# Layer 0 front: rotated q stored once and doubled by its load, keys of both heads in one transpose, v split two blocks at a time, retention scores on 128 rows

## The chip, the cores and the metric

The kernel runs on one core of a Trainium2 chip. The metric is the device time of one execution in microseconds (us). The engines are TensorE (PE; its weight loads are PEld), VectorE (DVE), ScalarE (ACT), GpSimd (POOL) and SyncE (SP, which here only issues DMAs). Work of one engine runs in the order of its queue; engines wait for one another through semaphores.

## The reference

A two-layer encoder on two sequences, 1024 and 512 tokens of 1024 features, all float32: twelve blocks of 128 tokens in all. Layer 0 has two branches from one projection, layer 1 has windowed attention. Only layer 0 is touched here:

```python
z = rmsnorm(x, g) @ w_in
qa, ka, va, ga, qb, kb, vb, gb = split(z)          # 512,128,128,512 | 256,256,512,512 columns
# mixer A: 8 query heads, 2 key/value heads, dim 64, dense attention
qa = rotate_pairs(rmsnorm(qa per head, gain0), ang) * 64**-0.5
ka = rotate_pairs(rmsnorm(ka per head, gain1), ang)
oa = softmax(qa @ ka.T) @ va                       # per head
# mixer B: retention, 4 heads, key dim 64, value dim 128, chunks of 128 tokens
s  = (qb @ kb.T) * decay                           # inside a chunk
ob = rmsnorm(s @ vb + (qb * q_decay) @ state)      # forward and backward scans summed
x  = x + concat(silu(ga) * oa, silu(gb) * ob) @ w_out
```

## The kernel before, in words

Tokens are taken in blocks of 128, four blocks make a group (three groups), two blocks a pair (six pairs). Products that need float32 accuracy are made from a high and a low part (`split`, L109 to L118: ACT writes the high part, DVE the rest).

**Order.** The program first loads x and projects keys and values of mixer A for all twelve blocks (`kv_raw`, tiles `zkv` of tag E). Then for each pair it runs eight pieces of the q projection of head group 0 (`q_pieces_a`), `kv_pair` for the rotary embedding of the keys, and after every second pair `kv_group`. Mixer B (`retention`, `retain`) follows, four heads by two sequences, twelve parts of four blocks. Attention of mixer A (`pipeline`, `prep_a`, `front_a`) comes last, with the q projection of head group 1, the bias table and the gates as filler (`fill_a`). In the filler the q tiles `zq` are taken from the gate weights' ring (`stage`, tag `wg`, four buffers); in the front they come from tag E. The program is laid out by a planner that simulates the engines (`schedule_with_timeline_sim=True`) and so chooses the order of each engine's queue; DMAs named here go through SP's queue but for the loads of split keys and values, which POOL issues.

**Rotary step.** `rope_norm` squares a pair on ACT, sums it on DVE (L389), makes 1/rms on POOL (L103), scales on DVE (L391), multiplies by the swapped sine on POOL (L394, two instructions), by the cosine on DVE (L397), and adds the two on DVE (L400). For q the caller hands in the outputs: for each of the two blocks, `qd` tiles of tag Q in which each head's 64 columns stand twice, so a pair has four adds of 128x256, and each block is stored as 512 columns (L448). For keys there are two adds of 128x128.

**Attention's q.** `prep_a` loads one block of 512 columns (L725), transposes four 128x128 squares, so that rows 0 to 63 and 64 to 127 hold the same query, and splits them into `qh` and `ql`. The key tile holds the high part on one half of its rows and the low part on the other, so that one product sums over both. There are 24 units, the loads in order of the units.

**Keys and values.** `kv_group` does each key/value head by itself: four transposes of a 128x64 slice into a PSUM tile, ACT and DVE make the high and low keys, and for each block one ACT copy and one DVE subtraction of 128x64 split v. Results go to DRAM (L470).

**Retention scores.** For each part `qk` (q beside k) is transposed by four transposes; ACT copies rows 0 to 63 to `qT` and rows 64 to 127 to `kT` (L555, L556), both tiles of 64 rows, and the score product `pss` runs with 64 rows of the array; `kv` and `po` products use 128.

Of the kernel before, what the change touches and what calls it, by code (L numbers as in the profile page):

```python
# [8 lines left out]
F32 = mybir.dt.float32  # L9
# [27 lines left out]
def trunk_kernel(ctx, tc, x, xT, wab, woab, wc, woc, gT, qkg, ret, sink, relb, fng,  # L37
# [15 lines left out]
    def buf(tag, name, n=None, dt=F32):  # L53
        t = wk.tile([P, SIZE[tag]], dt, tag=tag, name=name, bufs=BUFS[tag])
        return t if n is None else t[:, :n]
# [4 lines left out]
    def ps_t(name):  # L60
        return pp.tile([P, 512], F32, tag="s", name=name, bufs=5)
# [107 lines left out]
    def transpose(o, i):  # L169
        return nc.tensor.transpose(o, i, ident)  # L170
# [163 lines left out]
    x1T_d, x2T_d = scratch("x1T"), scratch("x2T")  # L334
    q_d = [[dr.tile([P, 512], F32, name=f"qd{g}_{b}")[:] for b in range(NB)] for g in range(2)]
    brow_d = dr.tile([16, 512], F32, name="browd")[:]
# [3 lines left out]

# [1 line left out]
    ident = const.tile([P, P], F32, name="ident")  # L342
# [20 lines left out]

# [1 line left out]
    dma(out=g_sb, in_=gT)  # L365
# [18 lines left out]

    def rope_norm(z, tb, nh, pos, tab, outs):
        tb = tb.rearrange("p (b h d) -> p b h d", b=2, h=nh)
        nc.scalar.activation(tb, z, AF.Square)
        ss = small("ssa", 8)[:, :2 * nh]
        nc.vector.tensor_reduce(ss.rearrange("p (b h) -> p b h", b=2), tb, AX.X, ALU.add)  # L389
        r = rstd_of(ss, 64, 2 * nh).rearrange("p (b h) -> p b h", b=2)  # L390
        nc.vector.tensor_tensor(z, z, r.unsqueeze(3).to_broadcast([P, 2, nh, 64]), ALU.mult)  # L391
        cosb, sinb = tab[:, 0, pos:pos + 2, :], tab[:, 1, pos:pos + 2, :]
        for f in range(2):
            nc.gpsimd.tensor_tensor(  # L394
                tb[:, :, :, f * 32:f * 32 + 32], z[:, :, :, (1 - f) * 32:(2 - f) * 32],
                sinb[:, :, f * 32:f * 32 + 32].unsqueeze(2).to_broadcast([P, 2, nh, 32]), ALU.mult)
        nc.vector.tensor_tensor(z, z, cosb.unsqueeze(2).to_broadcast([P, 2, nh, 64]), ALU.mult)  # L397
        for j in range(2):
            for o in outs(j):
                nc.vector.tensor_tensor(o, z[:, j], tb[:, j], ALU.add)  # L400

# [29 lines left out]
    def q_pieces_a(g, w, tab, filler):  # L431
        for p in PAIRS if filler else range(NB // 2):
            b = 2 * p
            ps = (ps_p if filler else ps_any)("psq")
            for j in range(2):
                for k in range(KT):
                    proj_tm_k(ps[:, j * CW:(j + 1) * CW], w, b + j, k)
                    if k % 2 and (j, k) != (1, KT - 1):
                        yield
            z, tb = stage("zq") if filler else (buf("E", "zq"), buf("H", "tbq"))  # L440
            for j in range(2):
                nc.scalar.activation(z[:, j * CW:(j + 1) * CW], ps[:, j * CW:(j + 1) * CW], AF.Copy,
                                     scale=rs[:, b + j:b + j + 1])
            qd = [buf("Q", "qdw").rearrange("p (h c d) -> p h c d", h=4, c=2) for _ in range(2)]
            rope_norm(z.rearrange("p (b h d) -> p b h d", b=2, h=4), tb, 4, b % 8, tab,
                      lambda j: [qd[j][:, :, c, :] for c in range(2)])
            for j in range(2):
                dma(out=q_d[g][b + j], in_=qd[j].rearrange("p h c d -> p (h c d)"))  # L448
            yield

    def kv_pair(p):
        z = kv_raw[p]
        for j in range(2):
            nc.scalar.activation(z[:, j], z[:, j], AF.Copy, scale=rs[:, 2 * p + j:2 * p + j + 1])
        k = z[:, :, 0]
        rope_norm(k, buf("H", "tbk", 256), 2, (2 * p) % 8, rk, lambda j: [k[:, j]])

    def kv_group(t):
        for i in range(2):
            kk, vv = (buf("Q", n, None, F32R) for n in ("ks", "vs"))  # L460
            pt = ps_t("ptk")
            for j in range(GB):
                z = kv_raw[(t * GB + j) // 2][:, j % 2]
                transpose(pt[0:64, j * P:(j + 1) * P], z[:, 0, i, :])
                vb = vv[:, j * P:(j + 1) * P]
                nc.scalar.activation(vb[:, 0:64], z[:, 1, i, :], AF.Copy)
                nc.vector.tensor_tensor(vb[:, 64:128], z[:, 1, i, :], vb[:, 0:64].bitcast(F32), ALU.subtract)
            split(kk[0:64], kk[64:128], pt[0:64], None)
            for n, v in (("ak", kk), ("av", vv)):
                dma(out=group((sp_d[n, i, 0], sp_d[n, i, 1]), t), in_=v.bitcast(F32))  # L470
# [26 lines left out]

# [1 line left out]
    ropeb = buf("S4", "ropeb").rearrange("p (f b d) -> p f b d", f=2, b=8)  # L499
# [22 lines left out]
    def retention(h, w, b0, b1):  # L522
# [7 lines left out]
        for i0 in parts:  # L530
# [21 lines left out]
            for j in range(GB):  # L552
                transpose(pt[:, j, :], qk[:, j, :])
            qT, kT = v4(buf("H", "qT"))[:64], v4(buf("H", "kT"))[:64]
            nc.scalar.activation(qT, pt[0:64], AF.Copy)  # L555
            nc.scalar.activation(kT, pt[64:128], AF.Copy)  # L556
            qfb = v4(buf("Q", "qfb"))
            for i in range(2):
                nc.vector.tensor_tensor(qfb[64 * i:64 * i + 64], qT,
                                        qdec[:64, h, i, :].unsqueeze(1).to_broadcast([64, GB, P]), ALU.mult)  # L560
# [59 lines left out]

# [1 line left out]
    class Back:  # L622
# [50 lines left out]
    def pipeline(units, prep, front, cap, frees, rate, fill, hook, before=None):  # L673
        """Software pipeline: the scores of later units run beside the products of this one, as far as
        the buffers of the exponentials (cap of them) reach."""
        n = len(units)
# [45 lines left out]
    def prep_a(u):  # L722
        g, b = u
        qd = buf("Q", "qd")
        dma(out=qd, in_=q_d[g][b])  # L725
        pt = ps_t("ptq")
        for h in range(4):
            transpose(pt[:, h * P:(h + 1) * P], qd[:, h * P:(h + 1) * P])
        qh, ql = buf("Q", "qh", None, F32R), buf("Q", "ql", None, F32R)
        split(qh, ql, pt, None)  # L730
        return qh, ql
# [70 lines left out]

# [1 line left out]
    def fin_fm(t, k, y, rb):  # L804
# [47 lines left out]

# [1 line left out]
    wkv = load_w(wc, 0, "w")  # L854
# [38 lines left out]

# [1 line left out]
    k_c, v_c = {0: (KH, KL)}, {0: (V,)}  # L895
# [108 lines left out]

# [1 line left out]
    def fin_out(t, k, y, rb):  # L1006
# [128 lines left out]
```

## Time and the profile before

| what | value |
| --- | --- |
| median of three timed runs | 1546.78 us (1539.06 to 1547.49) |
| profiled execution: span from its first to its last instruction | 1541.9 us |
| PE busy | 1467.9 us (95%) |
| DVE busy | 1061.1 us (69%) |
| ACT busy | 714.0 us (46%) |
| POOL busy | 804.7 us (52%) |
| mean granted TensorE clock | 0.985 |

A timed run holds the span and what lies around it; the profiled execution's own time stands beside the timed runs only through its span, which is 4.9 us under their median. Busy shares are averages over stages with different limits, and matmuls are pipelined, so a busy PE need not be one at its peak. The granted clock is a share of 2.4 GHz: 0.5 is the lower level of 1.2 GHz.

### The profile page before, as it was taken

The numbers are of one execution on the slowest core, as the hardware profiler recorded it, in microseconds if no ns is written. First come the engines' busy times: TensorE is split into PE (matmuls) and PEld (weight loads), VectorE is DVE, ScalarE is ACT, GpSimd is POOL, SyncE is SP. The second block draws the span as 40 slices with busy tenths as digits, with TensorE's granted clock in tenths as the row PEclk, the third lists the DMA queues.
The fourth block names the chain that finished last, engine by engine and source line by source line (L and its number), as shares of the span: only waits on it lengthen the run. The fifth ranks groups of instructions, "written<-read, shape, count | busy, mean of one in ns | idle before, by whom it ended". The sixth has DMA issues, their size and how long they took to land.

```text
span 1541.9 us, 26034 instructions
## 1 busy us (share of the span) xinstructions
PE 1467.9 (95%) x8746; PEld 1277.2 (83%) x8746; DVE 1061.1 (69%) x2488; ACT 714.0 (46%) x1768; POOL 804.7 (52%) x1040
## 2 busy tenths in 40 slices
PE   7989999989999999999998999999999999988897
PEld 7988999987888888778777998888888888766677
DVE  6596455578667667877888327677777767898554
ACT  3632222245455555655653235556556556555102
POOL 7783334257456374887896414442522432567433
PEclk9998999999999999999999999999999999999999
DMA  9441011224421132654563422112213211567773
GB/s 334 155 154 52 19 45 49 64 85 140 138 73 59 48 110 73 217 166 130 153 218 115 124 78 78 52 57 56 80 49 93 61 53 52 169 211 235 242 247 123
DMA packets 112662, 179.54 MB, mean 116 GB/s; under 512 B 12880, under 2 KB 34000, under 8 KB 112528
## 3 DMA queue, kind: packets, MB, share of 16 engines
q1 hardware_dynamic: 110512, 172.37, 35.6%
q0 software_dynamic: 2016, 5.51, 1.2%
q8 instruction: 69, 1.13, 0.3%
q14 instruction: 65, 0.53, 0.1%
HBM read 125.63 MB, written 56.39 MB: 118 GB/s over the span
## 4 chain that ended last, share of the span: by engine, by line
PE 65%; DVE 12%; DMA 8%; POOL 5%; issue 4%; ACT 2%; SPq 1%; POOLq 0%; DVEq 0%; ACTq 0%
PE psg L89 16%; PE psq L89 10%; PE psb L89 8%; PE po L89 8%; PE pte L170 6%; PE pso L89 4%; PE sc L89 3%; PE s L89 3%; PE pskv L89 2%; DMA wraw<-in_woc 2%; DVE xl L118 1%; DVE w L137 1%; DVE nm L782 1%; DMA wraw<-in_woab 1%; DVE el L112 1%
## 5 line engine op out<-in xcount | busy, mean ns | idle before, releaser
L89 PE MATMUL psg<-xh,wg 128*128 128x512 f32 x768 | 261.6, 399 | 1.4 <-POOL wg L137 1.2
L112 DVE TENSOR_TENSOR el<-pte,eh 128x512 fp32r<-128x512 f32 x288 | 196.6, 684 | 56.7 <-ACT eh L111 29.6
L107 POOL TENSOR_SCALAR ec<-ec,rl 128x384 f32<-128x384 f32 (+1 forms) x192 | 109.0, 582 | 233.0 <-DVE rl L997 77.1
L111 ACT ACTIVATE eh<-pte 128x512 fp32r<-128x512 f32 x288 | 169.4, 596 | 119.6 <-PE po L89 66.4
L89 PE MATMUL pso<-xh,w 128*128 128x512 f32 x512 | 179.8, 409 | 9.8 <-DVE w L137 4.3
L89 PEld LDWEIGHTS psg<-xh,wg 128*128 128x128 f32 x768 | 143.7, 188 | 29.7 <-POOL wg L137 1.6
L107 POOL TENSOR_SCALAR e<-e,rl 128x512 f32<-128x512 f32 x160 | 114.6, 728 | 81.7 <-DVE rl L793 23.8
L89 PE MATMUL psg<-xl,wg 128*128 128x512 f32 x384 | 151.1, 393 | 0.0
L992 ACT ACTIVATE ec<-ec,nm 128x384 f32<-128x384 f32 (+1 forms) x192 | 109.6, 572 | 85.6 <-DVE nm L990 80.8
L790 ACT ACTIVATE e<-s,nm 128x512 f32<-128x512 f32 x160 | 108.9, 687 | 75.3 <-DVE nm L787 56.1
L136 POOL TENSOR_SCALAR w<-wraw 128x512 fp32r<-128x512 f32 x116 | 78.7, 680 | 117.7 <-DMA wraw<-in_woc 35.2
L782 DVE TENSOR_REDUCE nm<-s 128x1 f32<-128x512 f32 x160 | 107.5, 682 | 34.3 <-PE s L89 34.0
L89 PE MATMUL psq<-xh,w 128*128 128x512 f32 x384 | 130.1, 397 | 0.6 <-DVE oT L655 0.6
L89 PEld LDWEIGHTS pso<-xh,w 128*128 128x128 f32 x512 | 96.1, 191 | 34.7 <-DVE w L137 7.8
L986 DVE CUSTOM_DVE_ANT_0 ec<-sc,bias,sink_s 128x384 f32<-128x384 f32 (+1 forms) x192 | 105.2, 568 | 20.3 <-PE sc L89 17.4
L89 PE MATMUL pso<-xl,w 128*128 128x512 f32 x256 | 102.0, 399 | 3.3 <-DVE xl L118 3.3
L170 PEld LDWEIGHTS pte<-ident,e 128*128 128x128 f32 x640 | 78.4, 142 | 20.5 <-ACT e L790 1.7
L170 PE MATMUL pte<-ident,e 128*128 128x128 f32 x640 | 94.6, 275 | 0.8 <-ACT e L790 0.6
L137 POOL TENSOR_TENSOR w<-wraw,w 128x512 fp32r<-128x512 f32 x68 | 90.5, 1335 | 1.8
L89 PEld LDWEIGHTS psq<-xh,w 128*128 128x128 f32 x384 | 71.8, 188 | 14.4 <-PE po L89 0.9
L89 PEld LDWEIGHTS psg<-xl,wg 128*128 128x128 f32 x384 | 72.3, 188 | 13.2
L89 PE MATMUL pskv<-w,xh 128*128 128x256 f32 x384 | 73.3, 293 | 9.0 <-ACT xh L117 6.7
(225 smaller groups left out, 3981.8 us busy)
## 6 DMA issues: line engine op xcount, KB each, us to landing
wraw<-in_woab SPq DMA_DIRECT2D x48, 256.0 KB, 3.3
wraw<-in_woc SPq DMA_DIRECT2D x48, 256.0 KB, 3.6
wraw<-in_wab SPq DMA_DIRECT2D x44, 256.0 KB, 3.3
wraw<-in_wc SPq DMA_DIRECT2D x36, 256.0 KB, 3.2
xt<-in_xT SPq DMA_DIRECT2D x24, 256.0 KB, 5.3
xb<-in_x SPq DMA_DIRECT2D x24, 256.0 KB, 4.9
qd<-qdw SPq DMA_DIRECT2D x24, 256.0 KB, 2.0
qd<-qd SPq DMA_DIRECT2D x24, 256.0 KB, 3.1
```

The costliest lines, as they stand in the source:

```text
L89: i = nc.tensor.matmul(ps, lhsT=lhsT, rhs=rhs, start=start, stop=stop)
L107: nc.gpsimd.tensor_scalar(o, i, s, 1.0, ALU.mult, ALU.mult)
L111: nc.scalar.activation(hi, src, AF.Copy)
L112: nc.vector.tensor_tensor(lo, src, hi.bitcast(F32), ALU.subtract)
L118: nc.vector.scalar_tensor_tensor(lo, src, scale, hi.bitcast(F32), ALU.mult, ALU.subtract)
L136: nc.gpsimd.tensor_scalar(w[:, 0, :], raw, 1.0, 1.0, ALU.mult, ALU.mult)
L137: (lo or nc.gpsimd).tensor_tensor(w[:, 1, :], raw, w[:, 0, :].bitcast(F32), ALU.subtract)
L170: return nc.tensor.transpose(o, i, ident)
L782: nc.vector.tensor_reduce(nm2[:, c:c + 1] if nh == 2 else nm[:, h:h + 1], s, AX.X, ALU.max, negate=True)
L790: nc.scalar.activation(eh[c], ss[c], AF.Exp, bias=nm[:, h:h + 1], accum_out=l[:, h, c:c + 1])
L986: nc.vector.tensor_tensor_reduce(es[h][:, :nk], s, bias[h][:, bo:bo + nk], 1.0, sink_s[:, 4 * c + h:4 * c + h + 1], ALU.add, ALU.max, mx[: ...
L992: nc.scalar.activation(es[a][:, :nk], es[a][:, :nk], AF.Exp, bias=nm[:, a:a + 1], accum_out=l[:, a:a + 1])
```

## The change

Four edits, all in layer 0. (1) `rope_norm` adds in place, in one instruction for the whole pair. q is stored from its own tile as 256 columns a block, and `prep_a` loads it twice, into the two 64-column halves of each head. (2) `kv_group` transposes the keys of both heads of a block at once and takes one PSUM tile for both. The second head's high part now goes to rows 64 to 127 and its low part to rows 0 to 63. (3) v is split for two blocks by one ACT and one DVE instruction. (4) `qT` and `kT` have 128 rows: `qT` is the whole transposed tile (q above, k below), and the lower half of `kT` is set to zero by POOL, so that the scores are the same.

```diff
-    q_d = [[dr.tile([P, 512], F32, name=f"qd{g}_{b}")[:] for b in range(NB)] for g in range(2)]
+    q_d = [[dr.tile([P, CW], F32, name=f"qd{g}_{b}")[:] for b in range(NB)] for g in range(2)]
...
-    def rope_norm(z, tb, nh, pos, tab, outs):
+    def rope_norm(z, tb, nh, pos, tab):
...
-        for j in range(2):
-            for o in outs(j):
-                nc.vector.tensor_tensor(o, z[:, j], tb[:, j], ALU.add)
+        nc.vector.tensor_tensor(z, z, tb, ALU.add)
...
-            qd = [buf("Q", "qdw").rearrange("p (h c d) -> p h c d", h=4, c=2) for _ in range(2)]
-            rope_norm(z.rearrange("p (b h d) -> p b h d", b=2, h=4), tb, 4, b % 8, tab,
-                      lambda j: [qd[j][:, :, c, :] for c in range(2)])
+            z4 = z.rearrange("p (b h d) -> p b h d", b=2, h=4)
+            rope_norm(z4, tb, 4, b % 8, tab)
             for j in range(2):
-                dma(out=q_d[g][b + j], in_=qd[j].rearrange("p h c d -> p (h c d)"))
+                dma(out=q_d[g][b + j], in_=z[:, j * CW:(j + 1) * CW])
             yield
...
-        rope_norm(k, buf("H", "tbk", 256), 2, (2 * p) % 8, rk, lambda j: [k[:, j]])
+        rope_norm(k, buf("H", "tbk", 256), 2, (2 * p) % 8, rk)
 
     def kv_group(t):
+        ks = [buf("Q", "ks", None, F32R) for _ in range(2)]
+        vs = [buf("Q", "vs", None, F32R) for _ in range(2)]
+        pt = ps_t("ptk")
+        for j in range(GB):
+            z = kv_raw[(t * GB + j) // 2][:, j % 2]
+            transpose(pt[:, j * P:(j + 1) * P], z[:, 0].rearrange("p h d -> p (h d)"))
         for i in range(2):
-            kk, vv = (buf("Q", n, None, F32R) for n in ("ks", "vs"))
-            pt = ps_t("ptk")
-            for j in range(GB):
-                z = kv_raw[(t * GB + j) // 2][:, j % 2]
-                transpose(pt[0:64, j * P:(j + 1) * P], z[:, 0, i, :])
-                vb = vv[:, j * P:(j + 1) * P]
-                nc.scalar.activation(vb[:, 0:64], z[:, 1, i, :], AF.Copy)
-                nc.vector.tensor_tensor(vb[:, 64:128], z[:, 1, i, :], vb[:, 0:64].bitcast(F32), ALU.subtract)
-            split(kk[0:64], kk[64:128], pt[0:64], None)
-            for n, v in (("ak", kk), ("av", vv)):
+            r0, r1 = 64 * i, 64 - 64 * i
+            split(ks[i][r0:r0 + 64], ks[i][r1:r1 + 64], pt[r0:r0 + 64], None)
+            for p in range(2):
+                v = kv_raw[t * 2 + p][:, :, 1, i, :]
+                vb = vs[i][:, p * CW:(p + 1) * CW].rearrange("p (b s d) -> p b s d", b=2, s=2)
+                nc.scalar.activation(vb[:, :, 0], v, AF.Copy)
+                nc.vector.tensor_tensor(vb[:, :, 1], v, vb[:, :, 0].bitcast(F32), ALU.subtract)
+            for n, v in (("ak", ks[i]), ("av", vs[i])):
...
-            qT, kT = v4(buf("H", "qT"))[:64], v4(buf("H", "kT"))[:64]
-            nc.scalar.activation(qT, pt[0:64], AF.Copy)
-            nc.scalar.activation(kT, pt[64:128], AF.Copy)
+            qT, kT = v4(buf("H", "qT")), v4(buf("H", "kT"))
+            nc.gpsimd.memset(kT[64:128], 0.0)
+            nc.scalar.activation(qT, pt, AF.Copy)
+            nc.scalar.activation(kT[0:64], pt[64:128], AF.Copy)
...
         qd = buf("Q", "qd")
-        dma(out=qd, in_=q_d[g][b])
+        q4 = qd.rearrange("p (h c d) -> p h c d", h=4, c=2)
+        for c in range(2):
+            dma(out=q4[:, :, c, :], in_=q_d[g][b].rearrange("p (h d) -> p h d", h=4))
```

## Rows read from the trace of the kernel before

**Rows 1.** The page's busy times, share of the span and instructions by engine.

```profile
PE 1467.9 (95%) x8746; PEld 1277.2 (83%) x8746; DVE 1061.1 (69%) x2488; ACT 714.0 (46%) x1768; POOL 804.7 (52%) x1040
```

**Rows 2.** Windows: length, busy PE, PEld, DVE, ACT, POOL, granted clock, DMA share, GB/s.

```profile
70.00:116.00 46.00, 41.22 (x328) 39.98 (x327) 44.02 (x102) 15.59 (x50) 38.55 (x48) 0.96 0.43 144
116.00:130.00 14.00, 10.57 (x52) 9.68 (x51) 8.66 (x23) 4.41 (x12) 3.48 (x13) 0.65 0.15 57
...
160.00:200.00 40.00, 40.00 (x337) 39.48 (x337) 21.97 (x47) 9.09 (x18) 15.36 (x30) 1.00 0.15 45
...
330.00:340.00 10.00, 9.40 (x55) 8.91 (x55) 8.10 (x13) 2.56 (x6) 6.71 (x6) 0.74 0.36 111
```

**Rows 3.** Waits of PE from 60 to 130 us: total us, times, longest.

```profile
PE ptk L170 <- DVE zkv L400: 4.7, 4, 1.6
PE ptq L170 <- DVE vs L467: 2.2, 1, 2.2
PE kv L89 <- DVE kfb L549: 1.3, 1, 1.3
```

**Rows 4.** Chain that ended last, up to 420 us: start us, us, what.

```profile
70.92 1.43 DVE qdw L400 x4
...
322.06 1.67 DVE qdw L400 x5
...
324.33 1.00 DVE qdw L400 x3
...
359.29 1.76 DVE qdw L400 x4
...
367.88 2.22 DVE qdw L400 x4
```

**Rows 5.** DVE groups by shape, 60 to 125 us: busy us, mean ns, idle before.

```profile
L400 DVE TENSOR_TENSOR qdw<-zq,tbq 128x256 f32<-128x256 f32 x24 | 9.0, 433 | 0.1
L467 DVE TENSOR_TENSOR vs<-zkv,vs 128x64 fp32r<-128x64 f32 x24 | 5.8, 299 | 0.1
L397 DVE TENSOR_TENSOR zq<-zq,tab 128x512 f32<-128x512 f32 x6 | 5.7, 957 | 1.4 <-POOL tbq L394 1.3
...
L400 DVE TENSOR_TENSOR zkv<-zkv,tbk 128x128 f32<-128x128 f32 x12 | 4.2, 392 | 0.0
```

**Rows 6.** The same chain in mixer B, one part.

```profile
148.83 0.89 PE kv L89 x8
...
151.99 1.08 PE pss L89 x8
```

**Rows 7.** Waits of PE from 320 to 800 us, the longest.

```profile
PE pto L170 <- DVE on L591: 5.2, 1, 5.2
```

**Rows 8.** POOL's timeline: a memset of mixer B, a gate weight's split.

```profile
160.82 0.28 POOL L525 MEMSET stt<- 64x128 f32 x1 [0.98 <-PE po L89]
...
370.25 0.62 POOL L136 TENSOR_SCALAR wg<-wraw 128x512 fp32r<-128x512 f32 x1 [0.76 <-POOL e L107]
```

**Rows 9.** DMA: packets, MB, share in 353.5:356.3 and 345.5:347.8; then landing us.

```profile
q1 hardware_dynamic: 288, 0.13, 16.5%
...
q1 hardware_dynamic: 223, 0.42, 49.5%
...
qd<-qdw SPq DMA_DIRECT2D x24, 256.0 KB, 2.0
qd<-qd SPq DMA_DIRECT2D x24, 256.0 KB, 3.1
```

**Rows 10.** Timeline: q loads on SP's queue, their transposes on PE.

```profile
332.78 0.38 SPq L725 DMA_DIRECT2D qd<-qd  x1
338.43 2.56 SPq L725 DMA_DIRECT2D qd<-qd  x2
...
336.21 0.60 PE L170 MATMUL ptq<-ident,qd 128*128 128x128 f32 x4
341.33 0.63 PE L170 MATMUL ptq<-ident,qd 128*128 128x128 f32 x4
```

More of the change, by code (lines that the diff above doesn't have):

```diff
@@ L553, in retention @@
                 transpose(pt[:, j, :], qk[:, j, :])
-            qT, kT = v4(buf("H", "qT"))[:64], v4(buf("H", "kT"))[:64]
-            nc.scalar.activation(qT, pt[0:64], AF.Copy)
-            nc.scalar.activation(kT, pt[64:128], AF.Copy)
+            qT, kT = v4(buf("H", "qT")), v4(buf("H", "kT"))
+            nc.gpsimd.memset(kT[64:128], 0.0)
+            nc.scalar.activation(qT, pt, AF.Copy)
+            nc.scalar.activation(kT[0:64], pt[64:128], AF.Copy)
             qfb = v4(buf("Q", "qfb"))
             for i in range(2):
-                nc.vector.tensor_tensor(qfb[64 * i:64 * i + 64], qT,
+                nc.vector.tensor_tensor(qfb[64 * i:64 * i + 64], qT[:64],
                                         qdec[:64, h, i, :].unsqueeze(1).to_broadcast([64, GB, P]), ALU.mult)
```

## The prediction

> **What bounds the kernel now.** I read the busy times first [rows 1]. PE is busy 95% of the span, so a change can pay in three ways: by taking work off PE, by removing one of its few waits, or by keeping its clock up. Next come the windows [rows 2]. From 160 to 200 us, in retention, PE is busy for all 40.00 us at full clock: there only PE's own work counts. From 70 to 116 us it is different. DVE is busy 44.02 of 46 us and PE 41.22, so DVE sets the pace, and POOL with 38.55 us is not far behind. From 116 to 130 us PE idles and the granted clock is 0.65, that is, much of the stretch ran at 1.2 GHz; what PE did before that fall was to wait. PE's waits from 60 to 130 us sum to 4.7 + 2.2 + 1.3 = 8.2 us, every one for DVE: for the key adds (L400), the v splits (L467) and a product that stands behind them on DVE [rows 3]. The chain that ended last confirms it: it runs through DVE, with one pair's four q adds as a piece of 1.43 us [rows 4]; the front has six pairs. The same q adds of head group 1 are on the chain again between 322 and 370 us, in four pieces that sum to 1.67 + 1.00 + 1.76 + 2.22 = 6.65 us [rows 4]. PE's longest wait after 320 us, 5.2 us, is in that stretch, for a DVE instruction that was queued behind eight of these adds [rows 7], and the clock is 0.74 right after it [rows 2].
>
> **The change part by part.** The sum is made against the profiled execution.
>
> *Adds of q, front.* Four adds cost 1.43 us [rows 4]. One add of 128x512 is not in the trace in this form. Doubling the 128x256 spacing gives 0.72 us; the cosine product of the same shape and engine took 957 ns in the mean, stretched where POOL worked beside it [rows 5]. So a pair saves 0.47 to 0.71 us, six pairs 2.8 to 4.3; I take 3.9, nearer the doubling, because the 128x256 adds (433 ns mean) are hardly stretched. *Key adds:* twelve of 392 ns become six that cost what a 128x256 add costs, 433 ns [rows 5]: 4.7 less 2.6 is 2.1 at most; as such instructions overlap a little I take 1.3, floor 0.4. *v split:* 24 of 299 ns become twelve of 128x128, at 392 ns by the nearest row [rows 5]: 7.2 less 4.7 is 2.5; I take 1.9, floor 1.1. ACT loses twelve copies too, which costs nothing and gains nothing, since it is busy 15.59 of 46 us [rows 2].
>
> DVE loses 7.1 us in the front by this, bounds 4.3 to 8.9. The most that PE can get is its 8.2 us of waits [rows 3]. POOL has 46 - 38.55 = 7.5 us of room [rows 2], and the chain is not on DVE all the time, so I take 6.0 us. The twelve transposes saved shorten PE too, but where it waits that is nothing; if the waits are gone, twelve at 0.11 us (an eighth of the 0.89 us of eight passes, [rows 6]) make 1.3, which I leave to the upper bound. What is late next is POOL's 1/rms and sine products.
>
> *Clock after the front.* From 116 to 130 us, 35% of 14 us is 4.9 us lost to the lower level [rows 2]. If the gaps before it shrink enough, all comes back; if one remains that is long enough, none. I take half, 2.4, with 0 and 4.9 as ends.
>
> *Scores on 128 rows.* A part's eight `pss` passes take 1.08 us of the chain, eight `kv` passes of the same size on 128 rows 0.89 [rows 6]. I price the new form like `kv`: 0.19 for each of twelve parts is 2.3 us, and as PE is full there [rows 2] it comes through. Floor 0, if the spacing comes from something else than the rows; upper bound 3.4, with some 0.1 us at the entry of each. The ACT copy of 128 rows instead of 64 has the same 512 columns: nothing. The memset: POOL's nearest is 64x128 in 0.28 us [rows 8]; four times the columns make at most 1.1 us, and POOL is busy 15.36 of 40 us there [rows 2], so nothing while its queue has that room. Behind it in POOL's queue stand the sine products of the next part; without the cover it would cost up to 12 x 1.1 = 13 us, which needs PE to wait for each part, and PE waits for none there.
>
> *q adds of group 1.* Of the 6.65 us on the chain [rows 4], four pairs at 0.72 to 0.96 remain: 2.8 to 3.8 us gained, 3.3 taken. The other two pairs are off the chain: nothing. On the other side, `z` is now the source of the store. Its buffer in the gate weights' ring is free not after the add but when the store has landed, 2.0 us later [rows 9]. The last gate weight's split starts at 370.25, right after the last add ends at 370.10 [rows 4, 8]. With a shorter add ending near 368.7 and 2.0 us of store, and 0.1 for the issue, it starts at 370.8: 0.6 us lost, 2.0 at worst.
>
> *The loads.* The stores halve, off the path. A load becomes two DMAs of 512 pieces of 256 bytes. From the windows [rows 9], a 512-byte packet took 16.5% of 16 engines for 2.8 us over 288 packets, 26 ns, and a 2 KB packet 49.5% of 16 for 2.3 us over 223, 82 ns. Two DMAs make 66 packets an engine, semaphore writes included (16 of the packets of each DMA): 1.7 us at 26 ns against 9 x 82 = 0.7 now. The second issue adds 0.4 us [rows 10]. So landing is 1.4 us later; ends 0.8 (17 ns, on the line through both rows) and 5.1 (82 ns). I take 26 ns, the nearest row. Two loads are tight: issued at 332.78 and 338.43, transposed at 336.21 and 341.33 [rows 10], 3.4 and 2.9 us; one before them has about as much, the later ones more. As the second of these two landed within 2.9 us, say 2.5, the new one needs 3.9: PE would wait about 0.5 and 1.0, the earlier one 0.2. I take 1.0 us lost; the planner can move the rest behind filler.
>
> A rule speaks against this edit. The Trainium skill, page DMA: Bandwidth & Descriptors, section Specifications, puts the least transfer for full rate at 512 bytes; below it the DMA engine reads, modifies and writes. No row here has packets of 256 bytes of data, so no run shows it yet; by the rule the sum is that of the second rival below, by the row the one that follows.
>
> The sum: 6.0 + 2.4 + 2.3 + 3.3 - 0.6 - 1.0 = 12.4 us. 1541.9 - 12.4 = 1529.5 us of span; the span lies 4.9 us under the median of the runs shown, and with it the time is 1534 us.
>
> **The rivals.** 0.5% of 1546.78 is 7.7 us, which is about what a measurement of this kernel can tell from no change; so faster means under 1539.0, slower over 1554.5.
>
> *DVE is relieved and POOL or the latency of the chain holds the pace.* For it: POOL's room of 7.5 us is little more than what DVE gives up, and a pair's rotary step goes to and fro between both. Against: PE waits for DVE alone. Then the front gains about 2, the clock nothing, the rest 4.0: 6 us, 1541.
>
> *Small pieces cost twice.* If a 256-byte piece takes 52 ns, twice the nearest row, an engine needs 3.4 us, and landing is 3.1 us later, 5.6 after the issue. The three tight loads then make PE wait 1.9 + 2.2 + 2.7 = 6.8 us instead of the 1.0: 12.4 - 5.8 = 6.6, 1540 us. For it: the shape. Against: the engines are idle around those loads. It is the case that the rule of the Trainium skill, page DMA: Bandwidth & Descriptors, section Specifications, would make.
>
> *Slower: the planner's new order.* The change moves every instruction from 70 us on, and the planner lays all queues anew. What a bad order costs is seen at 325 us: one instruction of DVE behind eight adds, 5.2 us of PE [rows 7] and 2.6 us of clock after it (26% of 10 us, [rows 2]), 7.8 in all. One more such stall in attention leaves 4.6 of the gain, two end 3 us slower than before; from three on it is over the bound: 12.4 - 23.4, 1558 us. For it: the sum is only 0.8% of a run whose order is chosen by a simulation. Against: after 375 us PE's waits are few and short, filler stands ready, and the shorter adds remove what made the one stall.
>
> *More than the sum.* All 8.2 us of PE's waits, 4.9 of clock, 3.4 of scores, and most of the stall at 325 us: some 21 us, 1526.
>
> **How the numbers follow.** Forecast 0.52, with its own range 1527 to 1540; POOL or latency holds 0.20; small pieces cost twice 0.08; the planner's stalls 0.13 (0.10 of them beyond the bound, the rest within it); more than the sum 0.07. Faster: 0.48 of the forecast, 0.07, and 0.05 of the two rivals around 1540, 0.60. Slower: 0.10, and 0.03 for stalls on top of the POOL case, 0.13. Same: the other 0.27. The range is 1523 to 1550: it holds the forecast, both rivals near 1540, more than the sum, and one or two stalls.
>
> **What would show it.** In the profile after: one L400 add a pair of 0.7 to 0.95 us, six fewer key adds; PE waits from 60 to 130 us down from 8.2 to about 2 and the first `pss` some 6 us earlier or more; the clock from there on at 1.00, or still near 0.65 over some 14 us; `pss` pieces at 0.89 instead of 1.08; the first attention units 3 us earlier again relative to retention's end; q loads landing in about 4 us, and no PE wait on `ptq` over 1 us. Wrong it would be if POOL is busy without gaps from 70 to 110 us, if PE waits for the q loads, or if new waits of PE by the 5 us appear after 320 us.

## The result, and the profile after

The changed kernel takes 1532.28 us (median of five, 1528.44 to 1537.83) against 1543.35 us for the kernel before, timed beside it (five, 1539.06 to 1547.49): a ratio of 0.9929, 95% interval 0.9902 to 0.9955, some 11 us or 0.7% faster. Timed again with other versions it took 1534.73 us, ratio 0.9938 (0.9926 to 0.9951). The profiled execution took 1532.67 us with a span of 1530.9, so 1.8 us lie around the span; the span fell by 11.0.

First the page's busy times of the changed kernel, the counterpart of [rows 1].

```profile
PE 1457.4 (95%) x8734; PEld 1271.2 (83%) x8734; DVE 1045.1 (68%) x2434; ACT 714.1 (47%) x1756; POOL 809.5 (53%) x1052
```

PE has twelve passes less, DVE 54 instructions and 16 us, POOL the twelve memsets. The windows (length, busy PE, PEld, DVE, ACT, POOL, granted clock, DMA share, GB/s) answer to [rows 2]:

```profile
70.00:116.00 46.00, 41.60 (x343) 40.79 (x341) 39.50 (x71) 15.50 (x41) 43.99 (x55) 1.00 0.31 104
116.00:130.00 14.00, 11.19 (x94) 10.75 (x93) 12.06 (x30) 6.28 (x15) 3.29 (x11) 1.00 0.21 77
```

The two fullest engines of the front have changed places: DVE fell from 44.02 to 39.50 us of 46, POOL rose from 38.55 to 43.99. From 116 to 130 us the granted clock is 1.00 where it was 0.65. In the kernel before, PE was at the lower level of 1.2 GHz for the first 7 us of retention, after a stretch in which it was busy for 3.47 of 6.90 us, as its own windows show:

```profile
116.00:122.90 6.90, 3.47 (x20) 2.81 (x18) 4.50 (x11) 4.41 (x12) 2.18 (x9) 0.80 0.31 115
122.90:130.00 7.10, 7.10 (x33) 6.87 (x33) 4.16 (x12) 0.00 (x0) 1.30 (x5) 0.50 0.00 0
```

PE's waits from 60 to 130 us (us in total, times, longest), the counterpart of [rows 3]:

```profile
PE ptk L170 <- DVE zkv L398: 4.4, 4, 1.8
PE ptq L170 <- DVE qk L547: 1.7, 1, 1.7
PE kv L89 <- DVE kfb L550: 1.1, 1, 1.1
```

They sum to 7.2 us and not to the 2 that I expected; before they were 8.2. The chain that ended last shows what it runs over (start, us, what):

```profile
86.08 0.87 DVE zq L398
...
91.23 1.37 POOL tbk L394 x2
92.60 3.17 POOL wg L137 x2
95.78 1.86 POOL rstd L103
...
104.14 0.69 DVE zq L398
...
108.68 0.83 DVE zkv L398
```

A pair's q add is one piece of 0.69 to 0.87 us where four took 1.43 [rows 4]. But the chain now runs over POOL: sine products, the split of a retention weight that stands between them (L137, 3.17 us) and 1/rms. Summed over its pieces, POOL carries 12.85 us of the chain from 72.5 to 109.5; in the kernel before it was 4.96 us from 72.5 to 111. The DVE groups of 60 to 125 us (busy us, mean ns, idle before) answer to [rows 5]:

```profile
L397 DVE TENSOR_TENSOR zkv<-zkv,tab 128x256 f32<-128x256 f32 x6 | 5.3, 885 | 0.4 <-POOL tbk L394 0.4
...
L469 DVE TENSOR_TENSOR vs<-zkv,vs 128x128 fp32r<-128x128 f32 x12 | 4.6, 417 | 0.2
L398 DVE TENSOR_TENSOR zq<-zq,tbq 128x512 f32<-128x512 f32 x6 | 4.6, 764 | 0.1
...
L398 DVE TENSOR_TENSOR zkv<-zkv,tbk 128x256 f32<-128x256 f32 x6 | 3.3, 555 | 0.1
```

The q adds fell from 9.0 to 4.6 us, the v splits from 5.8 to 4.6, the key adds from 4.2 to 3.3: 6.5 us less, against the 7.1 of the prediction. At the same time the key's cosine product (L397), which the change doesn't touch, went from 474 to 885 ns in the mean; q's product on the same line went the other way, from 957 to 772 ns, and q's scaling (L391) from 943 to 777. What that depends on is taken up in the last section. In retention the same chain shows one part:

```profile
142.59 0.89 PE kv L89 x8
...
145.75 0.89 PE pss L89 x8
146.64 5.27 PE psb L89 x44
```

The piece of the scores takes 0.89 us, as `kv` does (before 1.08, [rows 6]). The 44 passes behind them take 5.27; in the kernel before the same piece, `psb` x44 at 153.07, took 5.47. How these two prices come about is shown with e3 and e4. POOL's timeline has the new memset, 0.52 us, between two sine products:

```profile
110.14 0.52 POOL L556 MEMSET kT<- 64x512 f32 x1
```

PE's waits from 304 to 739 us, attention, of which [rows 7] gave the longest:

```profile
PE pto L170 <- DVE on L593: 4.0, 1, 4.0
...
PE ptq L170 <- DMA qd<-qd: 1.3, 1, 1.3
PE s L89 <- DVE el L112: 1.1, 2, 0.9
PE po L89 <- DVE oT L657: 0.7, 1, 0.7
```

The stall of 5.2 us is one of 4.0. The other three are not among the waits of the kernel before in that stage. In turn one of its waits behind the adds, of 1.5 us, is gone:

```profile
PE po L89 <- DVE el L112: 1.5, 1, 1.5
```

The loads of q answer to [rows 9, 10]: a window of 325 to 327 us that holds small packets alone (989 packets, 0.25 MB), then the median times to landing (KB each, us), then SP's issues (ns least/median/most):

```profile
q1 hardware_dynamic: 989, 0.25, 54.1%
```

```profile
qd<-qd SPq DMA_DIRECT2D x48, 128.0 KB, 3.1
...
qd<-zq SPq DMA_DIRECT2D x24, 128.0 KB, 1.8
```

```profile
L729 SPq DMA_DIRECT2D qd<-qd x48: 523/617/5236, 281.7 to 717.2; - x48
```

54.1% of 16 engines for 2 us over 989 packets is 17.5 ns for one of 256 bytes, near the lower end (17 ns) that I had put down. A load lands in 3.1 us as before; its issue takes SP 0.62 us, twice a block, instead of 0.38 once.

### The profile page after: what moved, and what is told of

Its sections match the earlier page's. It is cut to its first block, busy times and chain, and to the rows that moved or that the text cites. A ratio compares the mean times of both kernels' runs of the same rounds, so it can differ in the third digit from the quotient of the medians.

```text
span 1530.9 us, 25958 instructions
## 1 busy us (share of the span) xinstructions
PE 1457.4 (95%) x8734; PEld 1271.2 (83%) x8734; DVE 1045.1 (68%) x2434; ACT 714.1 (47%) x1756; POOL 809.5 (53%) x1052
## 4 chain that ended last, share of the span: by engine, by line
PE 64%; DVE 12%; DMA 8%; POOL 5%; issue 4%; ACT 1%; SPq 0%; POOLq 0%; DVEq 0%; ACTq 0%
PE psg L89 16%; PE psq L89 10%; PE psb L89 8%; PE po L89 8%; PE pte L170 6%; PE pso L89 4%; PE sc L89 3%; PE s L89 3%; DMA wraw<-in_woc 2%; PE pskv L89 2%; DVE xl L118 2%; DVE el L112 1%; DVE w L137 1%; DVE nm L786 1%; DMA mo<-gab 1%
## 5 line engine op out<-in xcount | busy, mean ns | idle before, releaser
L996 ACT ACTIVATE ec<-ec,nm 128x384 f32<-128x384 f32 (+1 forms) x192 | 109.5, 572 | 83.7 <-DVE nm L994 75.8
L137 POOL TENSOR_TENSOR w<-wraw,w 128x512 fp32r<-128x512 f32 x68 | 90.1, 1330 | 1.7
L89 PEld LDWEIGHTS psg<-xl,wg 128*128 128x128 f32 x384 | 72.3, 188 | 13.4
L89 PEld LDWEIGHTS psq<-xh,w 128*128 128x128 f32 x384 | 71.8, 188 | 13.7
```

The lines of the kernel that those rows point to most:

```text
L89: i = nc.tensor.matmul(ps, lhsT=lhsT, rhs=rhs, start=start, stop=stop)
L137: (lo or nc.gpsimd).tensor_tensor(w[:, 1, :], raw, w[:, 0, :].bitcast(F32), ALU.subtract)
L996: nc.scalar.activation(es[a][:, :nk], es[a][:, :nk], AF.Exp, bias=nm[:, a:a + 1], accum_out=l[:, a:a + 1])
```

## The experiments

The stages below are read from the first and last starts of four tiles' products: start (to the first q product of group 0), front (from there to the first score product of retention), retention (to the first q product of group 1), attention (first to last q transpose). The q product of group 0 starts at 42.7 to 45.5 us from one profile to the next, with the same code before it, so sums over the span carry 2.5 us of that. One profile of each kernel; the changed kernel has two. In brackets stand, in us, the sum of PE's waits in the stage and the time lost to the clock there, which is (1 - granted clock) x length. In retention PE waits for nothing, so there it is the clock alone.

| kernel | median us | ratio to before (95%) | start | front (waits, clock) | retention (clock) | attention (waits, clock) | span |
| --- | --- | --- | --- | --- | --- | --- | --- |
| before | 1543.35 to 1545.31 | 1 | 42.9 | 80.0 (8.2, 3.1) | 165.2 (3.7) | 434.0 (15.3, 5.1) | 1541.9 |
| changed | 1532.28 | 0.9929 (0.9902 to 0.9955) | 45.4 | 75.3 (7.2, 0.0) | 157.7 (0.0) | 434.4 (14.8, 6.8) | 1530.9 |
| changed, again | 1534.73 | 0.9938 (0.9926 to 0.9951) | 42.9 | 75.5 (7.3, 0.2) | 159.1 (1.5) | 435.1 (16.3, 3.4) | 1531.2 |
| e1: edit 1 alone | 1537.62 | 0.9955 (0.9937 to 0.9973) | 45.5 | 77.9 (6.4, 2.5) | 164.2 (2.6) | 431.4 (12.3, 5.1) | 1536.6 |
| e2: edits 2, 3 alone | 1544.01 | 1.0004 (0.9991 to 1.0018) | 45.5 | 80.6 (8.8, 3.8) | 164.5 (3.0) | 435.6 (15.4, 5.1) | 1549.0 |
| e3: edit 4 alone | 1540.36 | 0.9973 (0.9961 to 0.9986) | 42.7 | 80.2 (8.6, 3.1) | 159.5 (2.1) | 436.7 (16.9, 5.1) | 1536.7 |
| e4: edits 1 to 3 | 1537.86 | 0.9968 (0.9953 to 0.9984) | 42.7 | 75.9 (7.2, 0.6) | 164.4 (2.8) | 432.2 (13.4, 3.4) | 1532.8 |
| e5: edits 1 and 4 | 1530.69 | 0.9912 (0.9890 to 0.9934) | 44.4 | 77.8 (6.6, 2.9) | 158.2 (0.5) | 431.1 (12.5, 5.1) | 1528.4 |
| e6: changed, doubled by the store | 1529.61 | 0.9893 (0.9867 to 0.9918) | 42.9 | 74.0 (4.7, 1.7) | 157.7 (0.0) | 429.0 (12.1, 1.7) | 1519.2 |
| e7: changed, POOL relieved | 1527.88 | 0.9891 (0.9872 to 0.9910) | 44.1 | 75.6 (6.5, 1.7) | 157.8 (0.0) | 432.2 (13.4, 5.1) | 1526.3 |
| e8: changed without edit 3 | 1534.89 | 0.9933 (0.9909 to 0.9957) | 44.5 | 77.4 (7.1, 2.7) | 158.4 (0.7) | 434.1 (14.0, 5.1) | 1532.1 |
| e9: changed, e6 and e7 | 1528.47 | 0.9897 (0.9882 to 0.9912) | 43.2 | 74.6 (5.4, 1.7) | 157.8 (0.0) | 432.1 (13.2, 5.1) | 1527.6 |
| e10: edits 1, 4, store of e6 | 1531.20 | 0.9921 (0.9907 to 0.9934) | 42.8 | 79.8 (7.5, 4.3) | 158.5 (0.9) | 431.8 (13.7, 3.4) | 1529.4 |
| e11: e10 and e7 | 1527.12 | 0.9892 (0.9878 to 0.9907) | 42.9 | 75.3 (6.1, 0.0) | 157.7 (0.0) | 432.1 (13.2, 5.1) | 1525.5 |

e1 to e4 ran on one chip, e5 to e8 on another, e9 to e11 and the changed kernel again on a third, each group with its own runs of the kernel before.

**Edit 1 alone.** Of the change only the in-place add, the single store and the two loads.

```diff
+        nc.vector.tensor_tensor(z, z, tb, ALU.add)
...
+                dma(out=q_d[g][b + j], in_=z[:, j * CW:(j + 1) * CW])
```

> Edit 1 alone: q and key adds in place, q stored once, two loads. Theory A (the front gains because DVE is relieved, and the clock after it comes back because PE's gaps shrink): DVE loses 5.2 of the 7.1 us, so the front from the first q product to the first score product is 3 to 4 us shorter, the granted clock from 116 to 130 us is 0.9 or more, score pieces stay at 1.08 us, and the time is 6 to 9 us under before. Theory B (the clock comes back because the score products no longer run on 64 rows): clock near 0.65 as before, time 3 to 5 us under before. Theory C (the small loads cost what the adds give): time within 2 us of before, with waits of PE for the q loads of 3 us or more.

By the ratio it gains 7.0 us (4.2 to 9.7), most of the whole. Its front is 2.1 us shorter. PE's waits in the front are 6.4 us by the sum of its rows, POOL is busy 42.57 of 46 us, the clock from 116 to 130 us is 0.76. So theory A has its time, but not by its way: the front gained 2.1 us for the 3 to 4 told, the clock is not at 0.9, and over the timed runs 20.5 us are lost to it where the kernel before beside it lost 21.1. The table puts another 1.0 in retention and 2.6 in attention, and 2.2 lie behind it. Theory C fell.

**Edits 2 and 3 alone.** Keys of both heads in one transpose, v for two blocks at once.

```diff
+            transpose(pt[:, j * P:(j + 1) * P], z[:, 0].rearrange("p h d -> p (h d)"))
...
+            split(ks[i][r0:r0 + 64], ks[i][r1:r1 + 64], pt[r0:r0 + 64], None)
```

> Edits 2 and 3 alone: keys of both heads in one transpose, v split two blocks at a time. Theory A: DVE loses 1.9 us, PE 1.3 us where it waits anyway; the front is 1 to 2 us shorter, the clock from 116 to 130 us stays near 0.65 or comes back in part, the time is 1 to 3 us under before. Theory B: the same front, clock near 0.65. A rival D, that the whole of the front's gain comes from the transposes and not from the q adds: the front 4 us shorter and the time 6 us or more under before.

No change: 1.0004; theory D fell. (The execution profiled was its slowest, 1550.83 us.) The front is 80.6 us against 80.0, and PE's waits from 60 to 130 us, shown here, are 8.8 us where they were 8.2. The time lost to the clock, (1 - clock) x span averaged over its timed runs, is 26.1 us, against 21.1 in the kernel before beside it. So what DVE is spared here shortens no wait of PE, and the time lost to the clock is 5 us more.

```profile
PE ptk L170 <- DVE zkv L400: 5.1, 3, 1.9
PE ptq L170 <- DVE qk L550: 2.6, 1, 2.6
PE kv L89 <- DVE kfb L553: 1.1, 1, 1.1
```

**Edit 4 alone, and the change without it.** e3 has 128 rows in the scores and nothing else, e4 all but that.

```diff
-            qT, kT = v4(buf("H", "qT"))[:64], v4(buf("H", "kT"))[:64]
+            qT, kT = v4(buf("H", "qT")), v4(buf("H", "kT"))
+            nc.gpsimd.memset(kT[64:128], 0.0)
...
```

> Edit 4 alone: retention scores on 128 rows with a zeroed half of the keys. Theory A: score pieces 0.89 instead of 1.08 us, 2.3 us over twelve parts, and nothing else: clock from 116 to 130 us near 0.65, time 2 to 3 us under before. Theory B (64 rows also hold the clock down): clock 0.9 or more there, retention 7 us shorter, time 6 to 8 us under before. If the memset held up POOL's sine products, PE would wait in retention, where it waited for nothing.

> The changed kernel with edit 4 undone: scores on 64 rows as before, edits 1 to 3 kept. Theory A: score pieces at 1.08 again, 2.3 us over twelve parts, clock from 116 to 130 us 0.9 or more as in the changed kernel; time 2 to 3 us over the changed kernel, 8 to 9 us under before. Theory B: clock down to 0.65 again, time 7 us over the changed kernel, 4 us under before.

e3 gains 4.2 us, e4 4.9, more than theory A gave to either. The two plans have the same order of passes here, so the chains of both can be laid side by side. e3, on 128 rows:

```profile
133.59 0.89 PE pss L89 x8
134.49 11.51 PE psb L89 x96
```

and e4, on 64 rows:

```profile
130.25 1.09 PE pss L89 x8
131.34 11.71 PE psb L89 x96
```

The 22 passes ahead take the same, 2.62 and 2.63 us. The piece of the scores is 0.20 longer on 64 rows, and the piece of 96 passes behind it 0.20 longer as well. The weight loads, one for each pass, show where these times lie. e3, then e4:

```profile
133.20 0.19 PEld L89 LDWEIGHTS psb<-w,xl 128*128 128x128 f32 x1
133.32 0.98 PEld L89 LDWEIGHTS pss<-qT,kT 128*128 128x128 f32 x8
134.21 0.30 PEld L89 LDWEIGHTS psb<-w,xh 128*128 128x128 f32 x2
```

```profile
129.85 0.19 PEld L89 LDWEIGHTS psb<-w,xl 128*128 128x128 f32 x1
130.18 0.96 PEld L89 LDWEIGHTS pss<-qT,kT 64*128 64x128 f32 x8
131.26 0.30 PEld L89 LDWEIGHTS psb<-w,xh 128*128 128x128 f32 x2
```

The eight loads take 0.98 us on 128 rows and 0.96 on 64: a pass on 64 rows is not slower. The time lies at the two changes of form. From the load ahead to the first of the scores there are 0.12 us in e3 and 0.33 in e4, from that one to the load behind the group 0.89 and 1.08. The chain books the first price to the scores and the second to the passes behind them. The Trainium skill, page TensorEngine Tiling (Array Packing), section Key Properties, says that changing the tiling mode drains TensorE. The trace agrees as far as each change of form costs about 0.2 us here; that this time is a drain is not shown.

Together the two changes make 0.39 us for a part. Retention holds eleven of the twelve score groups (the twelfth comes after the first q product of group 1), and it is 4.9 us shorter in e3 than in e4. Of this 0.7 is clock, by the brackets of the table, and 4.2 the scores: ten parts at 0.39 are 3.9, and the rest is the first part, which runs at the lower clock. Net of the clock, retention is 157.4 to 157.8 us in every kernel with 128 rows and 161.5 to 161.6 in every one with 64. e3 also has no PE wait at all between its first score product and group 1: the memset and the wider copy are hidden. The clock lost over the whole run, averaged over the timed runs as above, is 21.4 us in e3 and 17.8 in e4: the edits of the front bring 3.3 us of it back, edit 4 none, so theory B, by which the 64 rows hold the clock down, fell.

**Do the edits add up?** e5 leaves `kv_group` as it was before, e8 only its split of v, which is shown here against the changed kernel.

```diff
-            for p in range(2):
-                v = kv_raw[t * 2 + p][:, :, 1, i, :]
+            for j in range(GB):
+                v = kv_raw[(t * GB + j) // 2][:, j % 2, 1, i, :]
...
```

> Edits 1 and 4 without 2 and 3 (keys of each head transposed by themselves, v split block by block). The single edits gave -7.0 (edit 1), 0 (edits 2 and 3) and -4.2 us (edit 4), and the three first together -4.9. Theory F: the keys' and values' edits matter only beside the q adds, since they shorten the front from 77.9 to 75.9 us and keep the clock up there: this kernel is 2 to 5 us over the changed one, its front 77 to 79 us, clock 0.96 from 70 to 116 us. Rival G, that the single times simply add: -11 us against before, within 2 us of the changed kernel.

> The changed kernel with edit 3 undone: v split block by block, 24 ACT and 24 DVE instructions of 128x64 instead of twelve of 128x128. Theory A (DVE's relief counts): the front 1 to 2 us longer than 75.3, clock from 116 to 130 us may fall again, time 1 to 5 us over the changed kernel. Theory P (POOL sets the pace): front within 0.5 us, time within 1.5 us of the changed kernel.

e5 gains 13.6 us (10.2 to 17.0), not less than the whole change; e8 gains 10.4, as much. The single gains (7.0, none, 4.2) sum to 11.2, the whole brings 9.6 to 11.0: they add, as rival G has it, and edits 2 and 3 add nothing to the time. In the front they do something in company: 75.3, 75.5 and 75.9 us with them, 77.8 in e5. It is the clock and not the waits: PE waits 7.2 and 7.3 us with both and 6.6 in e5, but 0.0 and 0.2 us are lost to the clock against 2.9. Without edit 3 (e8) it is 2.7 again, with a front of 77.4, 2 us longer, though the time is the same. Why the clock holds in the changed kernel beside 7.2 us of waits is not shown. e5 makes its front good in attention, 431.1 us against 434.4 and 435.1, with the same loads. No one wait of PE accounts for it, but their sum does: 12.5 us against 14.8 and 16.3, in many small ones. Over the fourteen profiles attention roughly follows that sum (429.0 us with 12.1, 436.7 with 16.9). Why the order that the planner gave e5 has fewer of them was not found.

**The doubling on the side of the store.** q is stored twice in pieces of 256 bytes and loaded by one DMA with 2 KB a partition.

```diff
...
+                for c in range(2):
+                    dma(out=q4[:, :, c, :], in_=z[:, j * CW:(j + 1) * CW].rearrange("p (h d) -> p h d", h=4))
...
-        for c in range(2):
-            dma(out=q4[:, :, c, :], in_=q_d[g][b].rearrange("p (h d) -> p h d", h=4))
+        dma(out=qd, in_=q_d[g][b])
```

> The changed kernel with the doubling moved to the store: each block is stored by two DMAs of 256-byte pieces into 512 columns and loaded by one DMA of 2 KB rows, as before. Theory L (the double load costs about 1 us, in PE's wait for a load near 310 us): 0 to 2 us under the changed kernel, PE's wait on the q load gone. Rival: a load issued as two costs SP's queue and the DMA engines more than that, 3 us or more under the changed kernel. Rival: the stores of small pieces hold the tile of q longer, so the kernel is 1 us or more over the changed one.

1529.61 us, ratio 0.9893, beside 0.9929 and 0.9938 for the loads doubled. (The execution profiled was its fastest, 1520.97 us, so its stages flatter it.) The page's DMA part shows the pieces now in the store:

```profile
qd<-zq SPq DMA_DIRECT2D x48, 128.0 KB, 2.4
...
qd<-qd SPq DMA_DIRECT2D x24, 256.0 KB, 3.3
```

PE waits for q loads 0.3 us, against 1.3 and 0.6 in the two profiles of the changed kernel. That is 1.0 at most of the 5 to 7 us between the ratios; the rest is not at the loads. So the rival's 3 us or more came as a time, but not by what the rival named.

**POOL relieved.** In the changed kernel, ACT instead of POOL makes the high parts of head 1's retention weights, whose low parts are the L137 piece of the chain above.

```diff
...
-            nc.gpsimd.tensor_scalar(w[:, 0, :], raw, 1.0, 1.0, ALU.mult, ALU.mult)
+            if act:
+                nc.scalar.activation(w[:, 0, :], raw, AF.Copy)
+            else:
+                nc.gpsimd.tensor_scalar(w[:, 0, :], raw, 1.0, 1.0, ALU.mult, ALU.mult)
...
-            ws.append(load_w(wab, h + 1, "w" if h % 2 else "wg"))
+            ws.append(load_w(wab, h + 1, "w" if h % 2 else "wg", act=h == 0))
```

> The changed kernel with the high part of the weights of retention head 1 (four copies of 128x512, 0.6 to 0.7 us each) on ACT instead of POOL; same values. In the changed kernel POOL is busy 43.99 of 46 us from 70 to 116 us and DVE 39.50. Theory P (POOL now sets the front's pace): POOL loses 2.7 us there, the front is 2 to 3 us shorter, 72.5 to 73.5 us instead of 75.3, the time 2 to 3 us under the changed kernel. Rival (the latency of the chain between POOL, DVE and ACT sets it, or DVE): front within 1 us, time within 1.5 us.

1527.88 us, ratio 0.9891. But the front, where the gain was to be, is 75.6 us: no shorter. Its window and PE's first wait:

```profile
70.00:116.00 46.00, 39.85 (x319) 39.25 (x318) 38.87 (x73) 18.06 (x46) 40.90 (x51) 0.96 0.32 104
```

```profile
PE ptk L173 <- DVE zkv L401: 6.1, 3, 2.5
```

POOL has 3 us less to do, its share of the chain is 6.4 us instead of 12.85, and PE still waits for the keys' adds: the chain now takes a weight's DMA instead (3.24 us at 94.86) and more of DVE. All of PE's waits in the front are 6.5 us where they were 7.2; the 0.7 gained went to the clock, of which the front lost 1.7 us here and 0.0 there. So POOL alone does not set the pace of the changed kernel's front. Neither theory came out: the front is not 2 to 3 us shorter, and yet the time is 4.4 under the changed kernel. The stages show 2.2 to 2.9 of it in attention, where PE's waits are 13.4 us against 14.8 and 16.3, and the rest behind it.

**Both, with and without edits 2 and 3.** The diffs are the two above, on the changed kernel (e9) or on e5 (e10, e11).

> The changed kernel once more, unaltered, beside the three that follow. Its place is to tell how much of a difference of 3 us between versions is spread: one profiled execution of it gave 1532.7 us, five timed ones 1528.4 to 1537.8. Every theory expects 1532 (1529 to 1535) and a ratio of 0.992 to 0.994 to the kernel before. A median of 1528 would mean that the gain of the version with head 1's high parts on ScalarE (1527.9) lies within the spread of the changed kernel.

> The changed kernel with both mendings: q doubled by two stores and loaded by one 2 KB row a partition, and head 1's high parts of the retention weights made by ScalarE. Theory S (the pieces of 256 bytes and the second load cost the attention stage about 4 us, and the relief of GpSimd is worth another 3 to 4): 1525 (1523 to 1527). Theory T (the relief of GpSimd was spread, the stores are what counts): 1529, as with the stores alone. Rival U (what the pieces of 256 bytes cost does not depend on the side they stand on): 1528 to 1532, and the attention stage, first to last q transpose, is 434 us again and not 429 to 431.

> Edits 1 and 4 alone, with q doubled by the store: no change in how keys and values are prepared. If the two edits on keys and values bring nothing in company either (theory V, from the 0 us they brought alone and the 1530.7 us without them), this is 1527 to 1530, as the changed kernel with the same stores. If they bring what the sum of the prediction gave them (rival W, about 3 us of the front and part of the clock), it is 3 us behind that one: 1532 to 1533, with PE waits of 3 us more between 60 and 130 us.

> Edits 1 and 4, q doubled by the store, and head 1's high parts on ScalarE: the candidate for the best version. Theory S with V: 1524 to 1526, the same as its sister with the edits on keys and values. Theory T with V: 1528 to 1530. Rival W: 1528, 3 us behind the sister.

On one chip: changed 1534.73 (1533.02 to 1535.44), e9 1528.47 (1527.70 to 1529.32), e10 1531.20 (1529.93 to 1534.02), e11 1527.12 (1526.07 to 1529.55). The mendings of e6 and e7 do not add: e9's ratio is that of each alone, so theory S fell. Theory T's 1529 and rival U's time fit e9, but U's attention of 434 us does not, it is 432.1. Theory T fell too, as e11 is 4.1 us faster than e10 and their runs do not overlap; there the relief of POOL is in the front, 79.8 to 75.3 us. Of these 4.5 us 1.4 are waits; the rest is PE's busy time, and 4.3 us were lost to the clock in e10's front and 0.0 in e11's. For e10 the time lies between theory V and rival W and nearer W: by the ratios it is 4.3 us behind e6, its front is 79.8 us against 74.0, and PE's waits there are 2.8 us more. W falls for e11, which is not behind e9. PE's waits in e10's front, the longest of them 4.0 us:

```profile
PE ptk L170 <- DVE zkv L398: 4.9, 3, 4.0
```

In the versions with edit 1, relief of DVE (edits 2 and 3) and relief of POOL do the same for the front: either brings it to about 75 us, and both together hardly more (74.6, 75.6). Much of that is the clock: without either relief 2.5 to 4.3 us of the front are lost to it (e1, e5, e10), with one or both 0.0 to 1.7 us; edit 2 alone beside edit 1 (e8) leaves 2.7. e9 and e11 beat both kernels, by 15.9 and 16.7 us against before and by 6.3 and 7.6 against the changed kernel beside them.

## Why the prediction came out

1534 us were predicted and 1532.28 measured, faster as the likeliest case said. The sum was 12.4 us of span, 11.0 and 10.7 came; the time around the span, taken as 4.9, is 1.8, and the two errors cancel in part. Term by term it is less good than the total, and that the total fits is in part luck: the front brought less than its term, scores and clock more than theirs, the adds of group 1 next to nothing, and 1.7 and 1.2 us came behind attention, where nothing was changed. The later start in the first profile, 45.4 us for 42.9, took 2.5 back. Two of the prediction's own signs of being wrong came true: POOL is busy for 39.16 of the 40 us from 70 to 110 (35.62 before), and PE waits 1.3 us for a load of q.

- **Front, 6.0 us taken, 4.7 and 4.5 came, and by another way.** The waits of PE, of which the prediction wanted 6 of 8.2 back, gave 1.0. The remaining 3.7 are PE's own busy time: the twelve transposes, 1.3 by my price, which I had left to the upper bound, and the clock inside the front, 0.94 from 70 to 100 us and 0.80 from 116 to 122.9 in the kernel before (1.8 and 1.4 us of lost clock, in part while PE idled), 1.00 now. The step that failed is "The most that PE can get is its 8.2 us of waits". DVE's own saving was sized well (6.5 for 7.1). That POOL's products are late next was right, and the rival in which POOL holds the pace came true as far as the waits go; e7 shows that relieving POOL hands the chain on. But that rival gave the clock nothing, and the clock is what came back.
- **Clock after the front, 2.4 with ends 0 and 4.9.** Retention is 7.5 and 6.1 us shorter. By its granted clock 3.7 us were lost there before, 0.0 and 1.5 after, so 3.7 and 2.2 of it are the clock, and 3.8 and 3.9 the scores. Averaged over the timed runs, 21.1 to 22.1 us are lost to the clock before, 16.2 and 17.8 after; these 3 to 6 us include the front's.
- **Scores, 2.3 with an upper end of 3.4; 3.8 and 3.9 came.** That the form of 64 rows costs PE time was right, the size was not. The step "0.19 for each of twelve parts" lays the price to the eight passes in their own form; they are spaced alike in both. What costs is the change into the form of 64 rows, and the change out of it costs 0.20 again, which stood in the chain of before as a longer piece behind the scores. The twelfth part lies behind retention and gained nothing there. The memset was rightly free (0.52 us, bound 1.1).
- **q adds of group 1, 3.3; next to nothing came.** The adds are as short as told, and the stall behind eight of them fell from 5.2 to 4.0. The others were on the chain at 359.29 and 367.88. Beside the first of them PE was busy for 1.90 of 1.90 us; beside the second it waited, the 1.5 us of the row above, and that wait is gone. But attention is 434.4 and 435.1 us against 434.0, for other waits came (1.3 + 1.1 + 0.7 in the rows above, and smaller ones), and the sum is 14.8 and 16.3 us where it was 15.3. The failed step is to count every add of the chain as a gain: shorter adds shortened the waits behind them, and the new order has others in their place. The hold of the gate weights' ring, 0.6, is not seen: the split that stood at 370.25 starts at 366.41.
- **Loads, 1.0; 1.3 and 0.6 came.** The packets were cheaper than taken (17.5 ns for 26) and landing did not lengthen; what is late is the issue. The rival of pieces that cost twice fell, for 256 bytes took 17.5 ns where 512 took 26. The Trainium skill, page DMA: Bandwidth & Descriptors, section Specifications, puts the least transfer for full rate at 512 bytes and says that below it the engine reads, modifies and writes. The trace agrees that 256 bytes run below full rate, at 14.6 bytes a ns against 25 for the 2 KB packets; the doubling was the prediction's own reading of it.
- **The planner's stalls.** No new stall of 5 us; the longest new wait after 300 us is the 1.3. But attention varies from 429.0 to 436.7 us over the versions with hardly any edit in it, which is as large as each of the prediction's terms and was no part of the sum.

Left open: why the planner's order leaves PE fewer small waits in attention in e5, e7 and e11 than in the changed kernel, and what makes the gain behind attention; and why the clock held in the changed kernel's front and not in those of e5 and e8.

## What to carry to other kernels

Price another form on PE at its two edges: here the passes themselves were spaced alike, and the change into the form and the change out of it cost some 0.2 us each. Where two engines pass a chain to and fro, work taken off the fuller one is worth only the distance to the next, so look at what the other will do before counting all of the waits as gain, and count what PE does itself, its clock included, apart from what it waits. A piece on the chain is a gain only if PE, too, has nothing else there. And read waits and lost clock stage by stage: a total can fit by errors that cancel.

## What was not expected of the hardware

Eight products on 64 rows were spaced as on 128 rows (0.96 and 0.98 us for eight weight loads), but the change into that form and the change out of it cost PE some 0.2 us each. A packet of 256 bytes took 17.5 ns of a DMA engine, one of 512 bytes 26, one of 2 KB 82. The issue of a load in 512 pieces took SP 0.52 us at least and 0.62 in the median, against 0.32 and 0.38 with 128 pieces. And a DVE product of 128x256 went from 474 to 885 ns in the mean with no edit to it. A fuller POOL does not explain that: in e5 the same product takes 507 ns with POOL busy for 43.93 of the same 46 us, in e4 882 with 40.73. With another order in DVE's queue other instructions are the long ones (q's product fell from 957 to 772 ns); what stretches them was not found.
